# Final norm's factors and the last rows' residual sums in PSUM instead of SBUF

## The chip, the cores and the metric

The kernel runs on one core of one Trainium2 chip. The metric is the device time of one execution in microseconds. A core has TensorE (PE; its weight loads are listed as PEld), VectorE (DVE), ScalarE (ACT), GpSimd (POOL), SyncE (SP, here only an issuer of DMAs), an on-chip memory SBUF of 128 partitions, and PSUM, which holds the results of TensorE in 8 banks of 512 float32 numbers per partition.

## The reference, cut to what matters

The model is one step of a two-layer streaming encoder: a gated short convolution, then multi-head latent attention, each with a norm before it and a residual add behind it, and one norm at the end. There are 1024 prompt frames and 64 sample frames, which the kernel handles as 1088 columns of width 1024. What the change touches is the end of layer 2, the residual sum and the final norm:

```
def rms_norm(x, g):
    y = x * rsqrt(mean(x * x, axis=-1) + EPS)
    return y * g

yp = (silu(zp) * op) @ mla_w_out      # 1024 x 1024
xp = xp + yp                          # residual sum
y_prompt = rms_norm(xp, final_norm_g) # the same for the sample frames
```

## The kernel before

Nearly everything is a float32 product made of three matmuls on operands that are split into a high and a low part (`hi`, `lo`): hi·hi, hi·lo, lo·hi. A weight block arrives by DMA (`wraw`, or `xraw`), ACT writes its high part (`whi`), and POOL subtracts to get the low part (`wlo`, or `xlo`); blocks 0 and 1 below have their lower half split between POOL and DVE.

The stage that matters is the last one, the output projection. It has two parts.

- Columns 0 to 831 are kept transposed, with the 1024 features in 8 groups of 128 partitions (`dt`), and in two column groups, (448, 832) and (0, 448). For every `dt`, PE makes one sum per column group in one of the four PSUM banks 0 to 3 that `gps()` hands out in turn, DVE adds the residual into `X2` (L1841), ACT squares it (L1846), DVE adds up the squares in `acc1` (L1848), and ACT multiplies `X2` by the norm's weight (L1853). After the last `dt`, the generator `finish` turns the summed squares into factors: PE sums over partitions with a matrix of ones, `wide_rstd` forms the factors rf (ACT Ln and Exp at L363 and L364, one correction step at L365 to L367), and then DVE multiplies all 8 slices of `X2` by rf (L1737) and SP sends each slice out (L1738). There are 8 multiplies of 384 columns and 8 of 448.
- The last 256 columns are computed the other way round, as rows: two blocks `b` of 128 frames, each in two halves `h` of 512 features, in the four PSUM banks 4 to 7 (`acc[b][h]`). Their weights come in 8 blocks `e`, 0 to 3 for the first half and 4 to 7 for the second. `rows(e, w, b)` issues 6 matmuls. Blocks 0 to 5 are used for both `b` one after the other; then come blocks 6 and 7 for b=0, then 6 and 7 for b=1. `half_end(b, h)` ends a half: DVE adds the residual that was copied to `XG` (L1803; for b=1, h=1 PE has added it already), ACT squares and sums it (L1805), DVE multiplies by the norm's weight (L1806). At h=1 follow the factor of each row (L1810 to L1815), the scaling on three engines (L1816, L1817, L1819), and the output DMAs.

Both parts run interleaved: `advance()` moves the open `finish` generators one step per weight block. The order on each engine is the one in which the program was laid out by its scheduler; engines wait for each other through semaphores and never change that order. PE's order is pinned to the program's. The high parts `whi` have two buffers, so block 7's high part takes the buffer of block 4 and can be written only when PE has finished with block 4.

Of the kernel before, what the change touches and what calls it, by code (L numbers as in the profile page):

```python
# [14 lines left out]
AF = mybir.ActivationFunctionType  # L15
# [4 lines left out]
D = 1024  # L20
# [189 lines left out]
def kernel(ctx, tc, xT, small, w1, w2, w3, w3r, wpair, wqr, wv, wkT, w4,  # L210
# [3 lines left out]
    V, A, G, PE, SP = nc.vector, nc.scalar, nc.gpsimd, nc.tensor, nc.sync  # L214
# [9 lines left out]
    def nm(s):  # L224
        cnt[0] += 1
        return f"{s}_{cnt[0]}"
# [9 lines left out]
    def gps(tag="g", size=1):  # L236
        (b0, b1), k = turns[tag]
        turns[tag][1] = (k + size) % (b1 - b0)
        return PS[:, b0 + k:b0 + k + size, :].rearrange("p b n -> p (b n)")
# [27 lines left out]
    def ordered(ins):  # L267
        if keep_order[0]:
            tc.keep_in_program_order(ins)
# [29 lines left out]
    def mm(ps, lhsT, rhs, start, stop, more=False):  # L299

        ins = PE.matmul(ps, lhsT, rhs, start=start, stop=stop, skip_group_check=more)  # L301
        if pe_order[0]:
            tc.keep_in_program_order(ins)
# [45 lines left out]
    def wide_split(hi, lo, acc, eps):  # L349

        ordered(A.activation(out=hi, in_=acc, func=AF.Identity, bias=eps))
        ordered(V.scalar_tensor_tensor(lo, acc, eps, r32(hi), op0=ALU.add, op1=ALU.subtract))

    def wide_sum(hi, lo, n, tag="g"):

        ps = gps(tag)[:, :n]
        mm(ps, onesr, hi, True, False)
        mm(ps, onesr, lo, False, True)
        return ps

    def wide_rstd(out, ps, n, t):

        tc.keep_in_program_order(A.activation(out=t, in_=ps, func=AF.Ln, scale=1.0 / n))  # L363
        tc.keep_in_program_order(A.activation(out=out, in_=t, func=AF.Exp, scale=-0.5))  # L364
        ordered(A.activation(out=t, in_=out, func=AF.Square))  # L365
        ordered(V.scalar_tensor_tensor(t, t, -0.5 / n, ps, op0=ALU.mult, op1=ALU.mult))
        ordered(V.scalar_tensor_tensor(out, t, 1.5, out, op0=ALU.add, op1=ALU.mult))  # L367
# [98 lines left out]
    def conv_mm(c, W, lag=0, mid=None):  # L466

        cs = slice(c * NS, (c + 1) * NS)
        wh, wl = W
        ps = gps()[:, :NS]  # L470
        for k in range(KD + lag):
            if k == KD // 2 and mid:
                mid()
            if k < KD:
                mm(ps, wh[:, k * P:(k + 1) * P], HS[:, k, cs], k == 0, False)
                mm(ps, wh[:, k * P:(k + 1) * P], LS[:, k, cs], False, False)
            if k >= lag:
                mm(ps, wl[:, (k - lag) * P:(k - lag + 1) * P], HS[:, k - lag, cs], False, k == KD + lag - 1)
        return ps
# [318 lines left out]
    for ct in range(STD):  # L798
# [70 lines left out]
        else:  # L869
            for pi, part in enumerate(PARTS):  # L870
# [4 lines left out]
                for c in range(2):  # L875
                    ps = conv_mm(c, W, (KD, 0)[c])
# [59 lines left out]
    for dt in range(KD):  # L936
# [5 lines left out]
        for c, (c0, c1) in enumerate(CHK):  # L942
            n = c1 - c0
            x = xr[c]
            ps = gps()
# [103 lines left out]
    def latent_mm(f, c):  # L1049
        c0, c1 = CHK[c]  # L1050
        if c == 0:
            lat[f] = load_w(w3[f], 1024)
        ps = gps("z")[:, :c1 - c0]
        xg(ps, *lat[f], c0, c1)
        return ps
# [39 lines left out]
    ps = latent_mm(2, 0)  # L1095
    q_rstd(1, sq1)
    latent_evac(2, 0, ps)
    ps = latent_mm(2, 1)
# [48 lines left out]
    for c, (c0, c1) in enumerate(CHK):  # L1147
        n = c1 - c0
        ps = gps("z")
# [115 lines left out]
    for g in range(4):  # L1265
# [3 lines left out]
        if g == 2:  # L1269
            ps = gps()  # L1270
# [405 lines left out]
    OS, W4 = {}, {}  # L1676
# [39 lines left out]
    GB = po.tile([P, D], F32, name="GB")  # L1716
# [7 lines left out]
    def finish(c0, c1, sq):  # L1724

        n = c1 - c0
        rf = acc1[:, c0:c1]
        V.tensor_add(rf, rf, sq)
        wide_split(*OS[c0, 0], rf, eps_sum[D])
        yield  # L1730
        if c0 == 0:
            yield
        t = po.tile([P, 512], F32, tag="sq", name=nm("sq"), bufs=3)
        wide_rstd(rf, wide_sum(*OS[c0, 0], n), D, t[:, :n])
        yield
        for dt in range(KD):
            (G if dt in () else V).tensor_mul(X2[:, dt, c0:c1], X2[:, dt, c0:c1], rf)  # L1737
            SP.dma_start(out=o_y[dt][:, c0:c1], in_=X2[:, dt, c0:c1])  # L1738
            if dt in (1, 3, 5):
                yield  # L1740
# [28 lines left out]
    acc = [[PS[:, 4 + 2 * b + h, :] for h in range(2)] for b in range(2)]  # L1769
    Y = [XG.rearrange("p d n -> p (d n)")[:, b * D:(b + 1) * D] for b in range(2)]  # L1770
# [26 lines left out]
            mm(acc[b][h], ol[:, bs], wh[:, kk], False, q == 3 and kk == 1)  # L1797

    def half_end(b, h):
        yh = Y[b][:, 512 * h:512 * h + 512]  # L1800
        s0, s1, v0, v, t, y = [ss[:, 8 * b + i:8 * b + i + 1] for i in range(6)]
        if b * h == 0:
            V.tensor_add(yh, acc[b][h], yh)  # L1803
        junk = po.tile([P, 512], F32, tag="sq", name=nm("sq"), bufs=3)
        A.activation(out=junk, in_=acc[b][h] if b * h else yh, func=AF.Square, accum_out=s1 if h else s0)  # L1805
        V.tensor_mul(yh, acc[b][h] if b * h else yh, GB[:, 512 * h:512 * h + 512])  # L1806
        if h == 0:
            V.tensor_scalar(v0, s0, 1.0 / D, EPS, op0=ALU.mult, op1=ALU.add)
            return
        A.activation(out=t, in_=s1, func=AF.Ln, scale=1.0 / D, bias=v0)  # L1810
        A.activation(out=y, in_=t, func=AF.Exp, scale=-0.5)
        V.scalar_tensor_tensor(v, s1, 1.0 / D, v0, op0=ALU.mult, op1=ALU.add)
        V.tensor_mul(t, y, y)
        V.scalar_tensor_tensor(t, t, -0.5, v, op0=ALU.mult, op1=ALU.mult)
        V.scalar_tensor_tensor(y, t, 1.5, y, op0=ALU.add, op1=ALU.mult)  # L1815
        A.activation(out=Y[b][:, 0:256], in_=Y[b][:, 0:256], func=AF.Copy, scale=y)  # L1816
        G.tensor_scalar(Y[b][:, 256:512], Y[b][:, 256:512], y, 1.0, op0=ALU.mult, op1=ALU.mult)  # L1817
        (A if b else SP).dma_start(out=o_t[b][:, 0:512], in_=Y[b][:, 0:512])
        V.tensor_scalar(Y[b][:, 512:1024], Y[b][:, 512:1024], y, None, op0=ALU.mult)  # L1819
        SP.dma_start(out=o_t[b][:, 512:1024], in_=Y[b][:, 512:1024])  # L1820
# [3 lines left out]
    for dt in range(KD):  # L1824
        if dt == 7:
            raw_load(0)
        if dt == 4:
            residual()
        if dt > 1:
            W4[dt] = load_w(w4[dt], 1024)  # L1830
        wh, wl = W4[dt]
        x1 = po.tile([P, 832], F32, tag="x1", name=nm("x1"), bufs=2)
        SP.dma_start(out=x1, in_=x1_d[dt][:, :832])
        for c0, c1 in GRP[0]:
            n = c1 - c0
            ps = gps()
            gemm(ps[:, :n],
                 lambda k: wh[:, k * P:(k + 1) * P], lambda k: wl[:, k * P:(k + 1) * P],
                 lambda k: OS[c0, k][0], lambda k: OS[c0, k][1], KD)
            xs = X2[:, dt, c0:c1]  # L1840
            V.tensor_add(xs, ps[:, :n], x1[:, c0:c1])  # L1841
            if dt == 0:
                A.activation(out=acc1[:, c0:c1], in_=xs, func=AF.Square)
            else:
                q = po.tile([P, 512], F32, tag="sq", name=nm("sq"), bufs=3)
                A.activation(out=q[:, :n], in_=xs, func=AF.Square)  # L1846
                if dt < KD - 1:
                    V.tensor_add(acc1[:, c0:c1], acc1[:, c0:c1], q[:, :n])  # L1848
                else:
                    fins.append(finish(c0, c1, q[:, :n]))  # L1850
                    for x in fins[::-1]:
                        next(x)
            A.activation(out=xs, in_=xs, func=AF.Copy, scale=sm[:, C_FG + dt:C_FG + dt + 1])  # L1853
# [4 lines left out]
    for e in range(8):  # L1858
        if e + 2 + 1 < 8:
            raw_load(e + 2 + 1)  # L1860
            w.append(raw_split())
        for b in range(2) if e < 6 else ():
            rows(e, w[e], b)
            if e == 3:
                half_end(b, 0)
        advance()
    for b in range(2):
        for e in (6, 7):
            rows(e, w[e], b)
        half_end(b, 1)  # L1870
# [90 lines left out]
```

## Time and profile before

| | |
|---|---|
| time, median of 3 runs | 1099.64 us (1098.98 to 1100.81) |
| profiled execution's own time | 1099.2 us |
| span of its profile | 1097.4 us |
| busy: PE, DVE, ACT, POOL | 95%, 69%, 58%, 48% of the span |

PE is busy almost all the time and its granted clock is full in nearly all of the 40 slices of the page; only the last slice stands clearly apart (PE 4 tenths busy, clock 7 tenths). A busy share is an average over all stages, so it tells nothing of that last slice; for it one reads the waits and the timelines of 1060 to 1097 us, instruction by instruction.

### The profile page before, as it was taken

How to read it: one execution, taken by the hardware profiler on the slowest of the kernel's cores; microseconds unless marked ns; L12 is line 12 of the kernel's file. 1: busy time of each engine (PE TensorE's matmuls, PEld its weight loads, DVE VectorE, ACT ScalarE, POOL GpSimd, SP SyncE). 2: the span in 40 equal slices, each digit the busy share in tenths (PEclk: the TensorE clock that was granted, in tenths of full speed). 3: DMA queues.
4: the chain of work that ended last, by engine and by line, in shares of the span. 5: the costliest groups of instructions: out<-in, count | busy, mean ns of one | idle time of the engine just before them, and what ended most of it. 6: DMA issues, size and time to landing. Idle time of an engine off the chain costs nothing.

```text
span 1097.4 us, 19670 instructions
## 1 busy us (share of the span) xinstructions
PE 1048.0 (95%) x7123; PEld 1003.3 (91%) x7123; DVE 754.0 (69%) x1523; ACT 638.3 (58%) x1388; POOL 532.1 (48%) x446
## 2 busy tenths in 40 slices
PE   9989998989999999999899999999999999989994
PEld 8979998989999999999798999899999999879983
DVE  6888666756666445555996432788888888896456
ACT  5446676666666533345522334877787778785352
POOL 0475698886576622113452322445555545563243
PEclk9999999999999999999998999999999999999997
DMA  7244232442323244422142114433422331334224
GB/s 236 69 129 147 88 124 92 134 153 84 116 79 114 82 151 140 133 99 80 53 139 104 34 50 115 104 80 87 109 57 66 88 90 47 103 120 150 89 85 155
DMA packets 58145, 114.55 MB, mean 104 GB/s; under 512 B 8080, under 2 KB 32400, under 8 KB 58048
## 3 DMA queue, kind: packets, MB, share of 16 engines
q1 hardware_dynamic: 57840, 112.97, 33.7%
q8 instruction: 56, 0.92, 0.4%
q14 instruction: 41, 0.34, 0.1%
q10 hardware_dynamic: 144, 0.26, 0.1%
q0 software_dynamic: 64, 0.07, 0.0%
HBM read 79.27 MB, written 16.31 MB: 87 GB/s over the span
## 4 chain that ended last, share of the span: by engine, by line
PE 69%; DVE 10%; POOL 5%; issue 5%; DMA 4%; ACT 4%; SPq 1%; POOLq 0%; DVEq 0%; ACTq 0%
PE PS L301 48%; PE PS L1487 16%; PE PS L1526 5%; DMA QB<-stg 3%; POOL wlo L1765 1%; DMA wraw<-in_w 1%; POOL wlo L292 1%; DVE PS L488 1%; ACT PH L1539 1%; DVE OL L1011 1%; ACT stg L1603 1%; POOL R L565 1%; SPq L1613 1%; DVE PL L1543 0%; POOL R L513 0%
## 5 line engine op out<-in xcount | busy, mean ns | idle before, releaser
L301 PE MATMUL PS<-R,whi 128*128 128x272 f32 (+2 forms) x1662 | 370.4, 313 | 15.4 <-ACT whi L288 4.4
L301 PEld LDWEIGHTS PS<-R,whi 128*128 128x128 f32 x1662 | 276.6, 191 | 20.1 <-ACT whi L288 5.1
L301 PE MATMUL PS<-R,wlo 128*128 128x272 f32 (+2 forms) x888 | 265.9, 311 | 1.2 <-POOL wlo L292 1.2
L292 POOL TENSOR_TENSOR wlo<-wraw,whi 128x1024 fp32r<-128x1024 f32 x36 | 88.7, 2465 | 185.5 <-ACT whi L288 179.6
L301 PEld LDWEIGHTS PS<-R,wlo 128*128 128x128 f32 x888 | 164.1, 190 | 2.4 <-POOL wlo L292 1.9
L1487 PE MATMUL PS<-KB,QB 96*128 96x512 f32 (+11 forms) x576 | 125.2, 355 | 1.1 <-DVE SZ L1031 0.6
L1521 POOL TENSOR_SCALAR Pt<-Pt,st 128x640 f32<-128x640 f32 (+3 forms) x64 | 61.4, 961 | 86.4 <-DVE st L1517 85.9
L1487 PEld LDWEIGHTS PS<-KB,QB 96*128 96x128 f32 (+1 forms) x576 | 94.4, 190 | 9.4 <-DVE PL L1543 1.1
L1504 DVE TENSOR_REDUCE st<-PS 128x1 f32<-128x1024 f32 (+7 forms) x128 | 94.7, 748 | 10.9 <-PE PS L1487 10.2
L1543 DVE TENSOR_TENSOR PL<-PS,PH 128x512 fp32r<-128x512 f32 (+3 forms) x192 | 98.7, 547 | 3.1 <-ACT PH L1539 1.8
L1539 ACT CAST PH<-PS 128x512 fp32r<-128x512 f32 (+3 forms) x192 | 85.4, 497 | 14.7 <-PE PS L1526 13.5
L1487 PE MATMUL PS<-PH,VB 128*128 128x256 f32 x320 | 76.5, 279 | 0.0
L637 POOL TENSOR_TENSOR wlo<-wraw,whi 128x1024 fp32r<-128x1024 f32 x26 | 62.5, 2404 | 27.1 <-ACT whi L636 24.2
L1487 PE MATMUL PS<-PL,VB 128*128 128x256 f32 x320 | 75.3, 282 | 0.2 <-DVE PL L1543 0.2
L1513 ACT ACTIVATE Pt<-PS,st 128x640 f32<-128x640 f32 (+3 forms) x64 | 62.1, 970 | 5.7 <-DVE st L1517 2.6
L301 PE MATMUL PS<-R,bhi 128*128 128x272 f32 x320 | 61.1, 289 | 2.6 <-DVE z L763 1.0
L1487 PEld LDWEIGHTS PS<-PH,VB 128*128 128x128 f32 x320 | 60.8, 190 | 1.3 <-DVE PL L1543 0.8
L1487 PEld LDWEIGHTS PS<-PL,VB 128*128 128x128 f32 x320 | 61.1, 191 | 0.7 <-DVE PL L1543 0.4
L288 ACT CAST whi<-wraw 128x1024 fp32r<-128x1024 f32 (+1 forms) x37 | 38.2, 1033 | 38.3 <-PE PS L301 20.6
L1526 PE MATMUL PS<-ident,Pt 128*128 128x128 f32 x416 | 55.4, 274 | 0.2 <-ACT Pt L1513 0.2
L301 PEld LDWEIGHTS PS<-R,bhi 128*128 128x128 f32 x320 | 49.6, 188 | 3.7 <-DVE z L763 1.2
L1568 POOL TENSOR_TENSOR SZ<-SZ,ot 64x256 f32<-64x256 f32 x64 | 47.0, 746 | 11.7 <-DVE ot L1563 9.4
(438 smaller groups left out, 2623.0 us busy)
## 6 DMA issues: line engine op xcount, KB each, us to landing
wraw<-in_w SPq DMA_DIRECT2D x83, 512.0 KB, 3.6
KB<-stg SPq DMA_DIRECT2D x32, 256.0 KB, 3.8
QB<-stg SPq DMA_DIRECT2D x32, 256.0 KB, 4.7
braw<-in_w SPq DMA_DIRECT2D x13, 512.0 KB, 4.4
QB<-qr_scratch SPq DMA_DIRECT2D x32, 128.0 KB, 3.1
x<-x_scratch SPq DMA_DIRECT2D x8, 416.0 KB, 3.2
xr<-in_xT SPq DMA_DIRECT2D x16, 192.0 KB, 2.4
x_scratch<-xr SPq DMA_DIRECT2D x16, 192.0 KB, 1.9
```

Source lines behind the costliest of these rows:

```text
L288: ins = A.copy(out=hi[:, :n], in_=raw[:, :n])
L292: ins = (lo_engine or G).tensor_sub(lo[:, :m], raw[:, :m], r32(hi[:, :m]))
L301: ins = PE.matmul(ps, lhsT, rhs, start=start, stop=stop, skip_group_check=more)
L637: ins = eng.tensor_sub(lo, src, r32(hi))
L1487: pin(PE.matmul(ps, lhsT, rhs, start=start, stop=stop))
L1504: pin(V.tensor_reduce(out=st[:, 0:1], in_=TL["S", h, i], axis=AX.XY, op=ALU.max, negate=True))
L1513: pin(A.activation(out=Pt, in_=TL.pop(("S", h, i)), func=AF.Exp, bias=st[:, 0:1], accum_out=st[:, 1:2]))
L1521: pin(G.tensor_scalar(Pt, Pt, st[:, 2:3], 1.0, op0=ALU.mult, op1=ALU.mult))
L1526: pin(PE.transpose(out=tp[:, j * P:(j + 1) * P], in_=TL["P", h, i][:, (j0 + j) * P:(j0 + j + 1) * P], identity=ident))
L1539: pin(A.copy(out=hi, in_=src))
L1543: pin(V.tensor_sub(lo, src, r32(hi)))
L1568: pin(G.tensor_mul(sz, sz, TL.pop(("ot", h, pr))[rows]))
```

## The change

In `finish`, the factors rf are no longer written over `acc1` in SBUF but into a PSUM bank of their own, one more call of `gps()` per column group. The 16 multiplies of `X2` then read one operand from SBUF and one from PSUM. In `half_end`, the residual sum of the three halves that need it is written back into its PSUM bank instead of into `XG`; the square and the multiply by the norm's weight read it there. No instruction is added or removed.

```diff
--- before.py
+++ after.py
@@ -1731,7 +1731,9 @@
         if c0 == 0:
             yield
         t = po.tile([P, 512], F32, tag="sq", name=nm("sq"), bufs=3)
-        wide_rstd(rf, wide_sum(*OS[c0, 0], n), D, t[:, :n])
+        ps = wide_sum(*OS[c0, 0], n)
+        rf = gps()[:, :n]
+        wide_rstd(rf, ps, D, t[:, :n])
         yield
         for dt in range(KD):
             (G if dt in () else V).tensor_mul(X2[:, dt, c0:c1], X2[:, dt, c0:c1], rf)
@@ -1797,13 +1799,13 @@
             mm(acc[b][h], ol[:, bs], wh[:, kk], False, q == 3 and kk == 1)
 
     def half_end(b, h):
-        yh = Y[b][:, 512 * h:512 * h + 512]
+        yh, ps = Y[b][:, 512 * h:512 * h + 512], acc[b][h]
         s0, s1, v0, v, t, y = [ss[:, 8 * b + i:8 * b + i + 1] for i in range(6)]
         if b * h == 0:
-            V.tensor_add(yh, acc[b][h], yh)
+            V.tensor_add(ps, ps, yh)
         junk = po.tile([P, 512], F32, tag="sq", name=nm("sq"), bufs=3)
-        A.activation(out=junk, in_=acc[b][h] if b * h else yh, func=AF.Square, accum_out=s1 if h else s0)
-        V.tensor_mul(yh, acc[b][h] if b * h else yh, GB[:, 512 * h:512 * h + 512])
+        A.activation(out=junk, in_=ps, func=AF.Square, accum_out=s1 if h else s0)
+        V.tensor_mul(yh, ps, GB[:, 512 * h:512 * h + 512])
         if h == 0:
             V.tensor_scalar(v0, s0, 1.0 / D, EPS, op0=ALU.mult, op1=ALU.add)
             return
```

The scheduler lays the instructions out nearly as before. On DVE, from the correction of the first factors to the residual sums of the first halves, the kernel before has (`sq` is the scratch of the correction, `acc` the factors, `X` is `X2`):

```order
L366 SCALAR_TENSOR_TENSOR sq_12072<-sq_12072,PS 128x384
L367 SCALAR_TENSOR_TENSOR acc_100<-sq_12072,acc_100 128x384
L1737 TENSOR_TENSOR X_11529<-X_11529,acc_100 128x384 x5
L366 SCALAR_TENSOR_TENSOR sq_12139<-sq_12139,PS 128x448
L1737 TENSOR_TENSOR X_11529<-X_11529,acc_100 128x384
L367 SCALAR_TENSOR_TENSOR acc_100<-sq_12139,acc_100 128x448
L1737 TENSOR_TENSOR X_11529<-X_11529,acc_100 128x384
L1737 TENSOR_TENSOR X_11529<-X_11529,acc_100 128x448 x2
L1803 TENSOR_TENSOR XG<-PS,XG 128x512 x2
```

and the changed kernel, with two lines more in its numbering:

```order
L366 SCALAR_TENSOR_TENSOR sq_12072<-sq_12072,PS 128x384
L367 SCALAR_TENSOR_TENSOR PS<-sq_12072,PS 128x384
L1739 TENSOR_TENSOR X_11529<-X_11529,PS 128x384 x4
L366 SCALAR_TENSOR_TENSOR sq_12139<-sq_12139,PS 128x448
L1739 TENSOR_TENSOR X_11529<-X_11529,PS 128x384
L367 SCALAR_TENSOR_TENSOR PS<-sq_12139,PS 128x448
L1739 TENSOR_TENSOR X_11529<-X_11529,PS 128x384
L1739 TENSOR_TENSOR X_11529<-X_11529,PS 128x448 x2
L1805 TENSOR_TENSOR PS<-PS,XG 128x512 x2
```

The first run of multiplies is one shorter, the multiply that left it stands behind the first halves' end; what stands in front of the two residual sums is otherwise the same, and the operand `acc` has become `PS`.

On ACT, the stretch from the high part of block 5 (`xhi`) to the first square of the second half reads in the kernel before (`whi_12179` is block 6's high part, `whi_12215` block 7's):

```order
L1763 CAST xhi_12153<-xraw_12151 128x1024
L1763 CAST whi_12179<-wraw_12177 128x1024
L1805 ACTIVATE sq_12190,ss<-XG 128x512
L1805 ACTIVATE sq_12201,ss<-XG 128x512
L1763 CAST whi_12215<-wraw_12213 128x1024
L1805 ACTIVATE sq_12264,ss<-XG 128x512
```

and in the changed kernel:

```order
L1765 CAST xhi_12153<-xraw_12151 128x1024
L1765 CAST whi_12179<-wraw_12177 128x1024
L1807 ACTIVATE sq_12190,ss<-PS 128x512
L1807 ACTIVATE sq_12201,ss<-PS 128x512
L1765 CAST whi_12215<-wraw_12213 128x1024
L1807 ACTIVATE sq_12264,ss<-PS 128x512
```

Nothing moved: the two squares of the first halves stand in front of block 7's cast in both, and read PSUM now. The orders of PE and POOL are unchanged. On the SP queue the output of the last but one 384-column slice stands behind four outputs of 448 columns instead of in front of them.

## Rows read from the trace of the kernel before

**Rows 1.** Waits by engine and releaser, 1060 to 1098 us: total, times, longest

```profile
PE PS L301 <- POOL wlo L1765: 4.7, 1, 4.7
PE PS L301 <- ACT whi L1763: 4.4, 1, 4.4
```

**Rows 2.** Stretches: busy us of PE, PEld, DVE, ACT, POOL; granted clock; DMA

```profile
1072.60:1075.40 2.80, 2.80 (x13) 2.06 (x11) 2.80 (x7) 0.00 (x0) 0.00 (x0) 1.00 0.55 204
...
1085.40:1089.00 3.60, 3.57 (x8) 2.81 (x9) 0.69 (x1) 0.31 (x1) 0.00 (x0) 0.50 0.00 0
```

**Rows 3.** Timeline of PE: start, duration, instruction, idle before and releaser

```profile
1070.99 0.39 PE L301 MATMUL PS<-whi,OL 128*128 128x512 f32 x1
...
1075.12 0.40 PE L301 MATMUL PS<-whi,OL 128*128 128x512 f32 x1
1079.93 0.80 PE L301 MATMUL PS<-whi,OH 128*128 128x512 f32 x1 [4.42 <-ACT whi L1763]
1085.43 0.79 PE L301 MATMUL PS<-wlo,OH 128*128 128x512 f32 x1 [4.70 <-POOL wlo L1765]
...
1087.30 0.63 PE L301 MATMUL PS<-whi,OL 128*128 128x512 f32 x1
```

**Rows 4.** Timeline of POOL, 1039 to 1100 us

```profile
1039.48 2.40 POOL L292 TENSOR_TENSOR wlo<-wraw,whi 128x1024 fp32r<-128x1024 f32 x1 [6.70 <-ACT whi L288]
...
1062.10 5.09 POOL L1765 TENSOR_TENSOR wlo<-wraw,whi 128x1024 fp32r<-128x1024 f32 x2 [2.58 <-ACT whi L1763]
1067.16 2.72 POOL L1765 TENSOR_TENSOR xlo<-xraw,xhi 128x1024 fp32r<-128x1024 f32 x1
...
1079.96 5.42 POOL L1765 TENSOR_TENSOR wlo<-wraw,whi 128x1024 fp32r<-128x1024 f32 x1 [7.41 <-ACT whi L1763]
```

**Rows 5.** Timeline of ACT, 1040 to 1100 us

```profile
1077.61 0.63 ACT L1805 ACTIVATE sq<-XG 128x512 f32<-128x512 f32 x1 [7.89 <-DVE XG L1803]
...
1078.85 1.03 ACT L1763 CAST whi<-wraw 128x1024 fp32r<-128x1024 f32 x1
...
1090.70 0.51 ACT L1816 ACTIVATE XG<-XG,ss 128x256 f32<-128x256 f32 x1 [0.73 <-DVE ss L1815]
1091.32 0.60 ACT L1805 ACTIVATE sq<-PS 128x512 f32<-128x512 f32 x1
```

**Rows 6.** Timeline of DVE, 1040 to 1100 us

```profile
1063.03 0.56 DVE L366 SCALAR_TENSOR_TENSOR sq<-sq,PS 128x384 f32<-128x384 f32 x1 [1.61 <-ACT sq L365]
1063.62 1.30 DVE L367 SCALAR_TENSOR_TENSOR acc<-sq,acc 128x384 f32<-128x384 f32 x1
1064.96 8.94 DVE L1737 TENSOR_TENSOR X<-X,acc 128x384 f32<-128x384 f32 x5
...
1076.89 1.28 DVE L1803 TENSOR_TENSOR XG<-PS,XG 128x512 f32<-128x512 f32 x2
...
1079.95 3.22 DVE L1737 TENSOR_TENSOR X<-X,acc 128x448 f32<-128x448 f32 x6
1087.96 0.69 DVE L1803 TENSOR_TENSOR XG<-PS,XG 128x512 f32<-128x512 f32 x1 [4.79 <-PE PS L301]
...
1092.04 0.69 DVE L1806 TENSOR_TENSOR XG<-PS,GB 128x512 f32<-128x512 f32 x1 [0.85 <-ACT sq L1805]
```

**Rows 7.** DVE groups by shape, 940 to 1098 us: total busy, mean ns

```profile
L1841 DVE TENSOR_TENSOR X<-PS,x 128x384 f32<-128x384 f32 x8 | 4.5, 556 | 6.4 <-PE PS L301 6.4
...
L1806 DVE TENSOR_TENSOR XG<-XG,GB 128x512 f32<-128x512 f32 x3 | 2.0, 685 | 0.8 <-ACT sq L1805 0.8
...
L1806 DVE TENSOR_TENSOR XG<-PS,GB 128x512 f32<-128x512 f32 x1 | 0.7, 692 | 0.9 <-ACT sq L1805 0.9
```

**Rows 8.** One line, L1543, 900 to 960 us: ns min/median/max

```profile
L1543 DVE TENSOR_TENSOR PL<-PS,PH x40: 271/610/693, 901.6 to 959.6; 128x512 fp32r<-128x512 f32 x20, 128x256 fp32r<-128x256 f32 x7, 128x384 fp32r<-128x384 f32 x7, 128x128 fp32r<-128x128 f32 x6
```

**Rows 9.** Timeline of the SP queue, 1062 to 1086 us

```profile
1064.54 0.37 SPq L1751 DMA_DIRECT2D wraw<-in_w  x1
```

**Rows 10.** DMA issues, 1035 to 1098 us: count, KB, us to landing

```profile
wraw<-in_w SPq DMA_DIRECT2D x4, 512.0 KB, 3.5
```

## The prediction

> **What bounds the kernel now.** PE is busy 95% of the span, so the end can come earlier only if PE loses idle time or if the work behind its last matmul gets shorter. I read the waits of the last 40 us first. PE waits twice and long: 4.4 us for block 7's high part and 4.7 us for its low part [rows 1]. [...]
>
> The timelines then tell why block 7 is late; I follow it backwards.
>
> - Its low part is a POOL instruction that starts at 1079.96 and takes 5.42 us; a lone one of that size takes 2.40 [rows 4]. The difference is 3.0 us, and from 1079.95 on DVE runs six multiplies in 3.22 us [rows 6]: POOL got through only behind them.
> - Its high part is cast at 1078.85, behind the squares of the two first halves on ACT, the first of which waited 7.89 us for DVE's residual sum [rows 5].
> - That sum starts at 1076.89, because DVE had five multiplies of 384 columns in front that took 8.94 us, 1.79 each, while POOL made low parts without a break from 1062.10 on [rows 4, 6].
>
> What makes these multiplies slow is seen in three neighbouring rows. The correction at 1063.03 reads one operand from PSUM and takes 0.56 us with POOL at work. The next, of the same size but with both tensor operands in SBUF, takes 1.30; then come the multiplies, both operands in SBUF too [rows 4, 6]. The same pair of engines loses time both ways: DVE waits in 1063 to 1073, POOL waits at 1080. With one operand in PSUM nothing of it shows: the forty subtractions of the attention stage never exceed 0.693 us, the time of their largest shape [rows 8]. The change puts exactly the second operand of these multiplies into PSUM.
>
> **The change part by part.** Times are those of the profiled execution.
>
> 1. First factors. The 384-column correction starts as before at 1063.03. Its second instruction falls from 1.30 to about 0.56: the multiplies start at 1064.22 instead of 1064.96.
>
> 2. Multiplies in front of the residual sums: six of 384, two of 448, and the other correction's two instructions of 448. A multiply of an SBUF and a PSUM tensor is not in this trace; the nearest row is the add of PSUM and SBUF at 384 columns, 0.556 us [rows 7]. Back to back, instructions overlap by some 0.08: two residual sums take 1.28 us, one takes 0.69; six multiplies take 3.22, which is 0.54 each [rows 6]. I take 0.47 for 384 (0.556 less 0.08) and 0.54 for 448: 6 x 0.47 + 4 x 0.54 = 5.0 us. The residual sums can start at 1069.2; PE is ready for them (block 3's last matmul starts 12 x 0.23 before 1070.99, so it ends at 1068.6 [rows 3]). Bounds: no row of these shapes is closer than 0.47 and 0.54, so these are the floor too; without any overlap it is 0.56 and 0.62, some 5.8 us, and if POOL holds them up as before it is 11.9 (1064.96 to 1076.89).
>
> 3. Block 7's high part. Before, the cast came 1.96 us behind the first residual sum (1078.85 less 1076.89). That gives 1071.2. But it also needs the buffer of block 4, whose last matmul ends at 1070.99 + 0.39 = 1071.38. So PE, not DVE, releases it, at 1071.45. Its data are there: the load is issued at 1064.54 and lands some 3.5 us later [rows 9, 10].
>
> 4. Block 7's low part. Cast 1.05, hand-over 0.06, then 2.40 on POOL with no SBUF-only DVE instruction beside it: ready at 1075.0.
>
> 5. PE. Block 6's last matmul for b=0 starts at 1075.12, the first of block 7 follows at 1075.35 and the second, which needs the low part, at 1075.58. That is 0.6 us after it is ready, so both waits vanish, and with them the slow clock. Block 7's sixth matmul starts at 1076.52 instead of 1087.30 and ends 0.39 later; the residual sum of b=0, h=1 starts at 1076.94 instead of 1087.96. **That is 11.0 us.**
>
> 6. Is DVE free by then? Behind the first two sums it has two multiplies by the norm's weight and eight of `X2`: 1.28 + 1.3 + 6 x 0.54 + 2 x 0.47 + 0.2 for two tiny ones, from 1069.2 to about 1076.1. Yes, by 0.8 us. The output DMAs of the multiplies follow them and are out of the way some 4 us before the last rows' outputs.
>
> 7. The end. From that residual sum on, the chain is the old one: sum, square, Ln, Exp, three short DVE steps, scaling, square of b=1 at 1091.32, and 6.08 us from there to 1097.4. PE's last twelve matmuls end 2.74 us behind block 7's sixth, at 1079.7, before ACT is free for that square (1091.21 less 11.0 is 1080.2), so the chain on ACT and DVE sets the end, and up to 0.1 us is gained there. The sum and the square in PSUM instead of SBUF cost nothing that rows show: 685 and 692 ns for the multiply of either kind [rows 7].
>
> [...] The new operands would let the weight multiply of a half run beside its square, since neither writes what the other reads. The row at 1092.04 shows such a pair already: both read one PSUM bank, and the multiply waits 0.85 us for the square all the same [rows 6]. [...]
>
> The sum: 1097.4 - 11.0 - 0.05 = 1086.3 of span, 1088.1 for the profiled execution (1099.2 before). The median of the runs lay 0.44 above that execution, so I carry the 11.1 us over to it: 1099.64 - 11.1 = 1088.5; between the two I write 1088.4.
>
> **The rivals.**
>
> *DVE becomes the bound.* If multiplies with a PSUM operand do not overlap, or pay some 0.1 to 0.2 us each, DVE finishes the sixteen late. With 0.2 more each it reaches the first sums at 1070.8, past the 1070.1 up to which block 7's low part is still in time, and ends its queue at 1079.3 instead of 1076.1: the last sum comes 2.4 us late. The two delays overlap, so the time is about 1090.8. For it: the price of this form is not in the trace. Against: two sums with a PSUM operand do overlap [rows 6]. Chance 0.12.
>
> *POOL still holds them up.* If it is the multiply's own tile, read and written in SBUF, that collides with POOL, the change does not do what it says. Everything from 1064.96 on stays, less the 0.7 us of the corrected factors, which the chain may or may not hand on: 1098.9 to 1099.6. Against: L1543 and the correction at 1063.03 also read and write SBUF. Chance 0.05.
>
> *PSUM reads slow down.* The factors lie in banks beside the ones that PE writes. If DVE's reads there were slowed, all sixteen multiplies would stand in front of the last sum: with m us each it starts at 1064.2 + 16 m + 3.9 (corrections, two sums, weight multiplies). At m = 1.24 that is 1087.96, no change; from 1.38 on it is over 0.2% later than now, and at 1.5 it is 1092.1, so the time is 1103.8. For it: no row has this form. Against: 1.38 is two and a half times the 0.556 of rows 7, whose adds also read PSUM while PE writes the neighbour banks. Chance 0.03.
>
> **How the numbers follow.** The forecast has 0.80 and a range of its own of 1087.0 to 1089.6: down by the overlap in step 7 and half a microsecond of scatter, up by a block 7 that misses its 0.6 us of slack by a little. The range takes in the first rival: 1086.6 to 1091.5, which leaves out some 0.13. About 0.2% (2.2 us) is what a measurement can tell from no change. Faster: 0.80 + 0.12 = 0.92; same 0.05; slower 0.03.
>
> **What would show it.** In the new profile the 384-column multiplies between 1064 and 1069 take about 0.56 us each and the POOL low parts 2.4, not 2.7; the first residual sums start near 1069.2; block 7's cast follows block 4's last matmul at 1071.4 and its low part ends by 1075.0; PE has no gap of over 1 us after 1062, and its clock stays at 1.00 to its last matmul near 1079.5; the sum of b=0, h=1 starts near 1077. Multiplies of 1.8 us beside POOL would refute step 2 and with it the forecast; a sum of b=0, h=1 released by DVE's own queue and not by PE would be the first rival.

## The result and the profile after

The changed kernel takes 1087.35 us at the median (1086.35 to 1089.01, 4 runs) against 1099.8 us (1098.98 to 1100.81, 4 runs) for the kernel before. The ratio is 0.9888 with a 95% interval of 0.9871 to 0.9905. The profiled execution took 1086.63 us, its span is 1084.8. One of the six runs of the kernel with the factors only, in the table below, took 1303.64 us at a granted clock of 0.721, where the others had 0.98 or more; it is left out of that kernel's numbers.

Start with DVE. This is its timeline in the changed kernel: start, duration, instruction, and the idle time before it.

```profile
1061.70 0.56 DVE L366 SCALAR_TENSOR_TENSOR sq<-sq,PS 128x384 f32<-128x384 f32 x1 [1.54 <-ACT sq L365]
1062.29 0.56 DVE L367 SCALAR_TENSOR_TENSOR PS<-sq,PS 128x384 f32<-128x384 f32 x1
1062.88 1.95 DVE L1739 TENSOR_TENSOR X<-X,PS 128x384 f32<-128x384 f32 x4
...
1066.28 1.61 DVE L1739 TENSOR_TENSOR X<-X,PS 128x384 f32<-128x384 f32 x3
1067.80 1.29 DVE L1805 TENSOR_TENSOR PS<-PS,XG 128x512 f32<-128x512 f32 x2
...
1070.85 3.67 DVE L1739 TENSOR_TENSOR X<-X,PS 128x448 f32<-128x448 f32 x7
1075.67 0.70 DVE L1805 TENSOR_TENSOR PS<-PS,XG 128x512 f32<-128x512 f32 x1 [1.15 <-PE PS L301]
1077.12 0.69 DVE L1808 TENSOR_TENSOR XG<-PS,GB 128x512 f32<-128x512 f32 x1 [0.75 <-ACT sq L1807]
```

The second instruction of the 384-column correction takes 0.56 us where it took 1.30, and four multiplies take 1.95 us, 0.49 each, where five took 8.94, 1.79 each [rows 6]. From the first multiply to the first residual sum it is 4.92 us instead of 11.93, with one multiply fewer in between. The groups by shape show where the gain lies (total busy, mean ns), first the changed kernel, then the kernel before:

```profile
L1739 DVE TENSOR_TENSOR X<-X,PS 128x448 f32<-128x448 f32 x8 | 4.6, 613 | 0.0
L1739 DVE TENSOR_TENSOR X<-X,PS 128x384 f32<-128x384 f32 x8 | 4.1, 548 | 0.0
```

```profile
L1737 DVE TENSOR_TENSOR X<-X,acc 128x384 f32<-128x384 f32 x8 | 10.6, 1362 | 0.0
L1737 DVE TENSOR_TENSOR X<-X,acc 128x448 f32<-128x448 f32 x8 | 4.6, 615 | 0.0
```

Only the multiplies of 384 columns were slow on DVE. Those of 448 were not: three ran while POOL was idle, and beside the six of [rows 6], five of them of 448 columns, it was POOL that lost time.

POOL's timeline: two low parts take 4.79 where they took 5.09, and block 7's, the last, takes 2.41 where it took 5.42 [rows 4].

```profile
1060.82 4.79 POOL L1767 TENSOR_TENSOR wlo<-wraw,whi 128x1024 fp32r<-128x1024 f32 x2 [2.58 <-ACT whi L1765]
1065.68 2.42 POOL L1767 TENSOR_TENSOR xlo<-xraw,xhi 128x1024 fp32r<-128x1024 f32 x1
1068.52 2.41 POOL L1767 TENSOR_TENSOR wlo<-wraw,whi 128x1024 fp32r<-128x1024 f32 x1 [0.41 <-ACT whi L1765]
1071.32 2.41 POOL L1767 TENSOR_TENSOR wlo<-wraw,whi 128x1024 fp32r<-128x1024 f32 x1 [0.39 <-ACT whi L1765]
```

ACT's timeline: block 7's cast comes 1.65 us behind the start of the first square and ends five microseconds before the next square, which waits for DVE's sum [rows 5].

```profile
1068.53 0.60 ACT L1807 ACTIVATE sq<-PS 128x512 f32<-128x512 f32 x1
...
1070.18 1.05 ACT L1765 CAST whi<-wraw 128x1024 fp32r<-128x1024 f32 x1 [0.37 <-issue]
1076.40 0.60 ACT L1807 ACTIVATE sq<-PS 128x512 f32<-128x512 f32 x1 [5.16 <-DVE PS L1805]
...
1078.37 0.51 ACT L1818 ACTIVATE XG<-XG,ss 128x256 f32<-128x256 f32 x1 [0.72 <-DVE ss L1817]
1078.79 0.58 ACT L1807 ACTIVATE sq<-PS 128x512 f32<-128x512 f32 x1
```

And PE, from block 4's last matmul to its own last one:

```profile
1069.71 0.39 PE L301 MATMUL PS<-whi,OL 128*128 128x512 f32 x1
...
1074.07 0.40 PE L301 MATMUL PS<-whi,OH 128*128 128x512 f32 x1
1074.30 0.39 PE L301 MATMUL PS<-wlo,OH 128*128 128x512 f32 x1
...
1075.24 0.39 PE L301 MATMUL PS<-whi,OL 128*128 128x512 f32 x1
...
1078.04 0.40 PE L301 MATMUL PS<-whi,OL 128*128 128x512 f32 x1
```

Block 7's first two matmuls follow each other after 0.23 us; both waits of [rows 1] are gone, and no matmul of the stage is at the slow clock of [rows 2], 0.50: from 1062.0 to 1078.4 the granted clock is 1.00. In the chain that ended last, followed from 1040 us on, PE's matmuls now reach without a break up to the residual sum of b=0, h=1 (start, length, what):

```profile
1039.84 35.81 PE PS L301 x169
...
1075.67 0.71 DVE PS L1805
...
1076.40 0.70 ACT sq L1807 x2
```

**How much of the 12.45 us is the change's?** The two profiles already stand apart in code that is the same in both: the 384-column correction starts at 1063.03 in one and at 1061.70 in the other. From that instruction to the end it is 34.37 us before and 23.10 after. So in these two profiles the last part is 11.27 us shorter. The other 1.33 us of the two spans lie ahead of it, where PE, DVE, ACT and POOL run the same instructions in the same order in both. Only ACT's last steps there write and read the factors in PSUM already, and DVE waits 1.54 us for them instead of 1.61 [rows 6]. The next section asks whether the rest is a gain. I call the part from the correction's start to the end of the span the last stretch and use it beside the times.

### The profile page after: what moved, and what is told of

The parts are those of the page before. It is cut to its first block, busy times and chain, and to the rows that moved or that the text cites. A ratio compares the mean times of both kernels' runs of the same rounds, so it can differ in the third digit from the quotient of the medians.

```text
span 1084.8 us, 19669 instructions
## 1 busy us (share of the span) xinstructions
PE 1045.5 (96%) x7123; PEld 1002.3 (92%) x7123; DVE 746.9 (69%) x1523; ACT 638.2 (59%) x1388; POOL 528.4 (49%) x446
## 4 chain that ended last, share of the span: by engine, by line
PE 74%; DVE 11%; ACT 4%; POOL 3%; DMA 3%; issue 3%; SPq 1%; POOLq 0%; DVEq 0%; ACTq 0%
PE PS L301 52%; PE PS L1487 17%; PE PS L1526 5%; DMA QB<-stg 2%; DVE PS L488 1%; POOL wlo L292 1%; DVE OL L1011 1%; ACT PH L1539 1%; ACT stg L1603 1%; POOL R L565 1%; POOL R L513 0%; DMA wraw<-in_w 0%; DVE qt L1212 0%; DVE SZ L367 0%; SPq L1613 0%
## 5 line engine op out<-in xcount | busy, mean ns | idle before, releaser
L1543 DVE TENSOR_TENSOR PL<-PS,PH 128x512 fp32r<-128x512 f32 (+3 forms) x192 | 98.7, 547 | 3.1 <-ACT PH L1539 1.8
```

The source lines that it names most:

```text
L1543: pin(V.tensor_sub(lo, src, r32(hi)))
```

## The experiments

The theory: a DVE instruction with two tensor operands in SBUF and a low part on POOL exclude each other; the multiplies lost their time so, and with the factors in PSUM they no longer do. The rivals: the factors' own place (they no longer overwrite `acc1`), the order on DVE, the residual sums, or a tile in SBUF that is slow in itself. Each kernel was timed against the kernel before on its own chip; the last stretch is from its profile.

| kernel | us, median | kernel before | ratio, 95% interval | last stretch, us |
|---|---|---|---|---|
| before | | | | 34.37 |
| changed | 1087.35 | 1099.8 | 0.9888 (0.9871 to 0.9905) | 23.10 |
| changed, again | 1086.1 | 1099.23 | 0.9875 (0.9853 to 0.9897) | 23.12 |
| factors only | 1088.72 | 1099.23 | 0.9899 (0.9874 to 0.9925) | 25.36 |
| sums only | 1099.34 | 1099.23 | 0.9997 (0.9982 to 1.0013) | 34.75 |
| factors in an SBUF tile of their own | 1099.56 | 1099.23 | 0.9996 (0.9981 to 1.0010) | 34.68 |
| order alone | 1095.53 | 1100.11 | 0.9961 (0.9947 to 0.9975) | 29.53 |
| PSUM for 384 columns only | 1094.39 | 1100.11 | 0.9946 (0.9933 to 0.9959) | 27.63 |
| POOL idle | 1093.1 | 1100.11 | 0.9937 (0.9919 to 0.9954) | 27.75 |
| changed, other ending | 1087.57 | 1100.11 | 0.9884 (0.9870 to 0.9898) | 22.85 |

**The changed kernel again**, without an edit.

> The changed kernel once more, for the distance to the kernel before on one chip and for the scatter of its unchanged part. Theory (the gain is the collision of VectorE and GpSimd on two SBUF operands, gone): about 11.3 us faster (10.96 us up to the residual sum of b=0, h=1 and 0.3 us behind it), so near 1088; the 384-column multiplies take 0.55 us each. The start of the 384-column correction (1063.03 in the profile before, 1061.70 in the first profile after) lies in unchanged code and is expected to differ by about 1 us from execution to execution. Rival (the other 1.3 us of the first result is a gain too): the correction starts at 1061.7 again and the gain is 12.4.

The last stretch is 23.12 us, the same to 0.02. But the correction started at 1065.28 this time, 3.6 us later than in the first profile. In the unchanged code such shifts come and go (1060.42 to 1065.28 over the ten profiles of this study), so one pair of profiles tells nothing of 1.3 us. On the mean the correction starts at 1062.9 in the five profiles with the 384-column factors in PSUM and at 1062.8 in the other five: no gain ahead of it shows. The times do not exclude one. This kernel is 13.13 us faster than the kernel before, where some 11.3 were expected, and the three timings with the whole change give 12.45, 13.13 and 12.54 us, all above 11.27, with intervals that begin at 10.4, 11.3 and 11.2. So 11.27 us are traced to the change; whether up to 2 us more are its work or scatter stays open.

**Factors only.** `half_end` is as before.

```diff
     def half_end(b, h):
-        yh, ps = Y[b][:, 512 * h:512 * h + 512], acc[b][h]
+        yh = Y[b][:, 512 * h:512 * h + 512]
...
-            V.tensor_add(ps, ps, yh)
+            V.tensor_add(yh, acc[b][h], yh)
...
```

> Only the final norm's factors go to PSUM; the last rows' sums stay in SBUF. Theory: the multiplies of X2 are as fast as in the changed kernel (0.55 us), so most of the gain is here. But the two weight multiplies of the first halves read XG and GB in SBUF, and now fall beside POOL's low part of block 6: DVE waits up to 1.4 us for it, then block 7's low part or the second weight multiply waits as well. So 0.2 to 2.3 us more than the changed kernel: 1088 to 1090. Rival (the two parts of the change are independent and the second is worth nothing): the same time as the changed kernel within 0.2 us and weight multiplies of 0.69 us.

The multiplies of 384 columns are as fast as in the changed kernel (0.546 us), but the last stretch is 2.26 us longer. DVE's and POOL's timelines show where:

```profile
1069.37 1.99 DVE L1808 TENSOR_TENSOR XG<-XG,GB 128x512 f32<-128x512 f32 x1
...
1071.34 2.83 DVE L1808 TENSOR_TENSOR XG<-XG,GB 128x512 f32<-128x512 f32 x1
...
1077.73 0.68 DVE L1805 TENSOR_TENSOR XG<-PS,XG 128x512 f32<-128x512 f32 x1
```

```profile
1068.40 2.41 POOL L1767 TENSOR_TENSOR wlo<-wraw,whi 128x1024 fp32r<-128x1024 f32 x1 [0.42 <-ACT whi L1765]
1071.20 2.42 POOL L1767 TENSOR_TENSOR wlo<-wraw,whi 128x1024 fp32r<-128x1024 f32 x1 [0.39 <-ACT whi L1765]
```

The weight multiplies of the first halves, both operands in SBUF again, take 1.99 and 2.83 us instead of 0.68. POOL's two low parts end at 1070.81 and 1073.62, and each multiply ends 0.55 us behind one of them, as if it had waited for POOL. Behind them DVE ends late, and the sum of b=0, h=1 starts at 1077.73, right behind DVE's own queue. So the second half of the change is worth 2.3 us, but only together with the first: it keeps a collision away that the earlier start of these multiplies would bring. The difference of the times, 2.6 us, goes the same way but lies within their intervals.

**Sums only.** The factors stay in `acc1`.

```diff
-        ps = wide_sum(*OS[c0, 0], n)
-        rf = gps()[:, :n]
-        wide_rstd(rf, ps, D, t[:, :n])
+        wide_rstd(rf, wide_sum(*OS[c0, 0], n), D, t[:, :n])
```

> Only the last rows' sums go to PSUM; the factors stay in acc1 in SBUF. Theory: the multiplies in front of the first residual sums still collide with POOL, 1.8 us each on the mean, and the first sums start some 13.8 us behind the correction as before: no change, 1099 to 1100. Rival (the sums carry part of the gain): 1 us or more faster.

No change, as the theory expected; here, as in the kernel before, the weight multiplies of the first halves meet an idle POOL and take 0.68 us each.

**Factors in an SBUF tile of their own.**

```diff
-        rf = gps()[:, :n]
+        rf = po.tile([P, 832], F32, tag="x1", name=nm("rf"), bufs=2)[:, :n]
```

> As the changed kernel, but the factors go into an SBUF tile of their own instead of a PSUM bank. Theory (PSUM matters): the multiplies take 1.8 us each beside POOL, the time is that of the kernel before, 1099 to 1100. Rival (what matters is that the factors no longer overwrite acc1, which other instructions use): the multiplies take 0.55 us and the time is 1087 to 1088.

The whole gain is gone, and the timeline of DVE is that of the kernel before:

```profile
1061.02 1.30 DVE L367 SCALAR_TENSOR_TENSOR rf<-sq,rf 128x384 f32<-128x384 f32 x1
1062.35 8.94 DVE L1739 TENSOR_TENSOR X<-X,rf 128x384 f32<-128x384 f32 x5
```

Five multiplies take 8.94 us once more. What counts is the memory, not that `acc1` is left alone.

**Order alone.** Everything in SBUF as before, but the multiplies wait for the residual sums of the first halves.

```diff
         wide_rstd(rf, wide_sum(*OS[c0, 0], n), D, t[:, :n])
         yield
+        for _ in range(3 if c0 else 1):
+            yield
         for dt in range(KD):
-            (G if dt in () else V).tensor_mul(X2[:, dt, c0:c1], X2[:, dt, c0:c1], rf)
+            with tc.issue_after(last_on["sum"]):
+                V.tensor_mul(X2[:, dt, c0:c1], X2[:, dt, c0:c1], rf)
...
-            V.tensor_add(yh, acc[b][h], yh)
+            last_on["sum"] = V.tensor_add(yh, acc[b][h], yh).ins
```

> Factors and sums stay in SBUF as before, but the sixteen multiplies are laid out behind the two residual sums of the first halves (they wait for the second of these), so that the squares and block 7's cast no longer queue behind them. Theory (two SBUF operands on VectorE and POOL's low parts exclude each other): block 7's cast comes as early as PE allows, but the multiplies then meet POOL's low parts of blocks 6 and 7 and one side waits for the other: either POOL for up to 8 us or DVE for 2.7 us per multiply. The end comes 3 to 9 us later than in the changed kernel: 1090 to 1096. Rival (only the order on DVE mattered, the squares behind the multiplies): as fast as the changed kernel, 1086 to 1088.

It gains 0.39%, about a third of what the changed kernel gains, and lies in the range of the theory. PE no longer waits for block 7 at all, but the collision has moved with the multiplies:

```profile
1071.22 2.77 DVE L1740 TENSOR_TENSOR X<-X,acc 128x448 f32<-128x448 f32 x1
1073.91 2.89 DVE L1809 TENSOR_TENSOR XG<-XG,GB 128x512 f32<-128x512 f32 x1
...
1076.79 7.57 DVE L1740 TENSOR_TENSOR X<-X,acc 128x448 f32<-128x448 f32 x15
1084.28 0.68 DVE L1806 TENSOR_TENSOR XG<-PS,XG 128x512 f32<-128x512 f32 x1
```

```profile
1070.79 5.45 POOL L1768 TENSOR_TENSOR wlo<-wraw,whi 128x1024 fp32r<-128x1024 f32 x2
```

One multiply takes 2.77 us and one weight multiply 2.89 beside POOL's last two low parts; the other fifteen run at 0.50 each as soon as POOL is through, but too late: the last sum waits for them until 1084.28. The order explains how the lost time reached PE, not why it was lost.

**PSUM for the 384-column factors only.**

```diff
-        rf = gps()[:, :n]
+        rf = gps()[:, :n] if c0 else rf
```

> As the changed kernel, but only the 384-column factors are in PSUM; the 448-column ones stay in acc1. Theory: the six 384-column multiplies in front take 0.55 us, so the first sum starts about 5 us behind the correction; the 448-column multiplies meet POOL's blocks 5 to 7 with both operands in SBUF and cost DVE or POOL 2 us apiece where they meet: 1.5 to 5 us later than the changed kernel, 1088 to 1092. Rival (the collision is met only by the multiplies in front of the first sums): the time of the changed kernel within 0.5 us.

The last stretch is 4.53 us longer than the changed kernel's, inside the 1.5 to 5 that were expected. The median of the times, 1094.39, lies 2.4 above the upper end that I gave. The profiled execution, 1091.86, does not, but it is the shortest of the five. I put the difference down to the scatter of the code ahead, without a profile that shows it. On DVE each kind shows its own price; POOL's lines stand below:

```profile
1063.65 2.41 DVE L1739 TENSOR_TENSOR X<-X,PS 128x384 f32<-128x384 f32 x5
...
1066.98 2.35 DVE L367 SCALAR_TENSOR_TENSOR acc<-sq,acc 128x448 f32<-128x448 f32 x1
...
1069.85 1.14 DVE L1739 TENSOR_TENSOR X<-X,acc 128x448 f32<-128x448 f32 x2
...
1072.18 5.08 DVE L1739 TENSOR_TENSOR X<-X,acc 128x448 f32<-128x448 f32 x2
```

```profile
1061.59 4.79 POOL L1767 TENSOR_TENSOR wlo<-wraw,whi 128x1024 fp32r<-128x1024 f32 x2 [2.58 <-ACT whi L1765]
1066.44 2.41 POOL L1767 TENSOR_TENSOR xlo<-xraw,xhi 128x1024 fp32r<-128x1024 f32 x1
1071.68 5.11 POOL L1767 TENSOR_TENSOR wlo<-wraw,whi 128x1024 fp32r<-128x1024 f32 x2 [2.83 <-ACT whi L1765]
```

Five multiplies with a PSUM operand take 2.41 us beside POOL. The one 448-column correction with both operands in SBUF takes 2.35 beside POOL, and two multiplies of that kind 5.08. Two more of the same kind, from 1069.85 on, fall into the gap in which POOL is idle and take 1.14 together.

**POOL idle.** Everything in SBUF as before, but DVE makes the low parts of blocks 3 to 7.

```diff
-        for eng, a, b in ((G, 0, 512), (V, 512, 1024)) if e < 2 else ((G, 0, 1024),):
+        for eng, a, b in ((G, 0, 512), (V, 512, 1024)) if e < 2 else ((V if e >= 3 else G, 0, 1024),):
```

> Factors and sums in SBUF as before, but the low parts of blocks 3 to 7 are made by DVE instead of POOL, so POOL is idle while DVE multiplies. Theory: the multiplies with both operands in SBUF take 0.55 us (384) and 0.61 us (448), none over 0.7, as there is nothing to collide with. DVE pays five low parts of 1.1 to 1.2 us for it, block 7's comes about 3 us too late for PE, and the time is 1089 to 1094. Rival (an SBUF factor tile is slow in itself in this stage, by its address or by PE's and DMA's traffic): the multiplies in front of the first sums still take 1.8 us on the mean.

This is the cleanest test, since the multiplies are the very same instructions as before (total busy, mean ns):

```profile
L1737 DVE TENSOR_TENSOR X<-X,acc 128x448 f32<-128x448 f32 x8 | 4.6, 618 | 0.0
L1737 DVE TENSOR_TENSOR X<-X,acc 128x384 f32<-128x384 f32 x8 | 4.2, 551 | 0.0
```

At 384 columns it is 551 ns with both operands in SBUF and POOL idle, 1362 ns in the kernel before with POOL at work, and 548 in the changed kernel with a PSUM operand and POOL at work. The SBUF factors are not slow in themselves. POOL's low parts both read and write SBUF, and no run has a POOL instruction there that does only one of the two, so which of them collides is not shown. The kernel pays for its low parts on DVE, as expected: PE waits 2.8 us for block 7's.

```profile
PE PS L301 <- DVE wlo L1765: 2.8, 1, 2.8
```

**Another ending.** In the changed kernel, DVE takes over ACT's and POOL's shares of the last scaling for b=0, and ACT takes over POOL's for b=1.

```diff
-        A.activation(out=Y[b][:, 0:256], in_=Y[b][:, 0:256], func=AF.Copy, scale=y)
-        G.tensor_scalar(Y[b][:, 256:512], Y[b][:, 256:512], y, 1.0, op0=ALU.mult, op1=ALU.mult)
+        if b:
+            A.activation(out=Y[b][:, 0:512], in_=Y[b][:, 0:512], func=AF.Copy, scale=y)
+        else:
+            V.tensor_scalar(Y[b][:, 0:512], Y[b][:, 0:512], y, None, op0=ALU.mult)
```

> The changed kernel with another sharing of the last scaling: for b=0 DVE scales all 1024 columns and ACT none, so that ACT is free for b=1's square when PE ends; for b=1 ACT scales 512 columns, DVE 512 and POOL none. Expected from the profile of the changed kernel: the square of b=1 starts at PE's end, 0.3 us earlier, and the last scaling ends 0.2 us earlier (0.61 us on ACT for 0.77 on POOL): 23.1 us from the correction to the end become 22.6, which the times cannot tell from no change. Rival: DVE's two scalings for b=0 stand in front of b=1's weight multiply and take the gain back: 23.0 to 23.2.

The last stretch is 0.25 us shorter, half of the 0.5 expected: the square of b=1 is released by PE now, but ACT's 512 columns take 0.72 us, not 0.61. The times cannot tell it from the changed kernel.

```profile
1080.32 0.60 ACT L1807 ACTIVATE sq<-PS 128x512 f32<-128x512 f32 x1 [0.82 <-PE PS L301]
...
1082.30 0.72 ACT L1819 ACTIVATE XG<-XG,ss 128x512 f32<-128x512 f32 x1 [0.72 <-DVE ss L1817]
```

## Why the prediction was right

The forecast was 1088.4 us, the median is 1087.35, inside the range and inside the forecast's own range of 1087.0 to 1089.6. The steps below explain 0.17 of the 1.05 us between the two; the rest is not in the sum. The second timing of the changed kernel, 1086.1, lies even under the range's lower end of 1086.6. So the mechanism was right, but how well the number fits is in part luck: runs of one kernel scatter by some microseconds. By its steps:

1. First factors: 0.56 us for the second instruction of the correction, as said.
2. Multiplies: 4.92 us up to the first sum for the 5.0 of the sum, 548 ns each for the 556 that I took from the nearest row. Here a PSUM operand cost nothing more: with one it is 548 ns, with two SBUF operands and POOL idle 551. They also overlap alike: in a row, each further one adds 0.47 us with a PSUM operand (four take 1.95) and 0.48 with two SBUF operands and POOL idle (two take 1.03). Why the multiplies were slow at all is told by DVE's rows beside POOL: 2.66 to 2.76 us with two SBUF operands, 0.55 with one. The multiplies, corrections and weight multiplies of all ten profiles divide in the same way: with one operand in PSUM none takes more than 0.69 us, beside POOL's low parts or not; with both in SBUF they take at most 0.69 us while POOL is idle and 1.28 to 2.89 beside a low part, or the low part loses the time, as beside the six of [rows 6].
3. Block 7's cast starts 0.08 us behind the end of block 4's last matmul, which is at 1070.10. The trace names no releaser for it ("issue"), so that this matmul releases it is read from the times; in the second profile of the changed kernel the distance is 0.08 us too.
4. Its low part: 2.41 us, ready at 1073.73.
5. PE reaches the matmul that needs it at 1074.30: 0.57 us of slack for the 0.6 forecast, no wait. From the correction to the sum of b=0, h=1 it is 13.97 us instead of 24.93: 10.96 for the 11.0 of the sum.
6. DVE is free 1.15 us before that sum, for the 0.8 that I worked out; the sum is released by PE, and the multiplies overlap, which excludes the first rival.
7. The end: mis-sized, if only a little. I gave up to 0.1 us; it was 0.31 (9.44 before and 9.13 after from the sum's start). Before, the square of b=1 still waited for PE, whose matmuls had been slow up to 1089 (granted clock 0.50 [rows 2]), and started 0.62 us behind the start of ACT's scaling [rows 5]. Now PE is done at 1078.44 and the square starts 0.42 us behind that scaling, at 1078.79, as soon as ACT lets it. That is 0.20 of the 0.31 us, where the working had counted 0.11; the other 0.11 are spread over the steps before and behind it. The weight multiply at 1077.12 waits 0.75 us for the square that reads the same bank, though neither writes it, and nothing was gained there; before it was 0.85 us [rows 6].

The sum is thus 11.27 us where I had 11.1. One thing the working did not see, though its number came out right: it priced the weight multiplies at 0.65 us each and said that sums in PSUM instead of SBUF cost nothing. Moved forward beside POOL's low parts they would have cost 2.3 us with the sums in SBUF, as the kernel with the factors only shows. The edit that I valued at nothing protects the gain of the other.

The two rivals on the far side are excluded by the multiplies' 548 ns. That POOL still holds them up would have shown as in the kernel with the factors in an SBUF tile of their own, and slow reads of PSUM beside PE's writes show nowhere.

## What to carry to other kernels

Where VectorE and GpSimd work at the same time, look at the operands of VectorE's long two-tensor instructions. Here, with both in SBUF, they and GpSimd's took turns; with one in a free PSUM bank they ran side by side, each as fast as alone (548 ns a multiply of 384 columns for 551 with POOL idle, 2.41 us a low part for 2.40). Follow the price through the queues before you judge it. An engine that is 69% busy lost some 7.2 us (three multiplies of 2.66, 2.76 and 2.74 us for 0.55 each, and a correction of 1.30 for 0.56), and POOL lost 3.0 behind six multiplies. That became 9 us of idle time and a slow clock (0.50) on the engine that sets the end, because a cast stood behind a square that stood behind a sum that stood behind the multiplies. And when work moves forward, check what it runs beside in its new place. The same collision still stands elsewhere in the changed kernel: the sum of squares of 448 columns at 1038.63 (L1850, both operands in SBUF) takes 2.45 us beside a POOL low part.

## What the runs showed of the hardware that was not expected

- The two engines did not yield alike. This is the line of the `X2` multiplies in the kernel before, while POOL has four low parts to make (ns min/median/max):

```profile
L1737 DVE TENSOR_TENSOR X<-X,acc x9: 546/615/2762, 1065.0 to 1076.4; 128x384 f32<-128x384 f32 x7, 128x448 f32<-128x448 f32 x2
```

  Most take 0.6 us, but three of the first five take 2.66 to 2.76, about the length of one POOL low part each, and three of POOL's four parts take 2.70 to 2.73 instead of 2.40: a waiting DVE instruction got in behind every POOL instruction and ended 0.4 us behind it. A waiting POOL instruction did not get in between six DVE multiplies that followed each other without a gap: block 7's low part took 3.0 us more than alone, about the length of the stream [rows 4, 6]. The two other kernels with this order on DVE show the same (5.45 us). This is read from the traces, not tried by itself.
- Two SBUF operands are not the only case. The last scalings on DVE (L1821 in the changed kernel, `TENSOR_SCALAR`) read one tensor in SBUF, and POOL scales its share beside them. From the kernel with POOL idle, whose last scalings POOL still shares:

```profile
1083.99 0.48 POOL L1817 TENSOR_SCALAR XG<-XG,ss 128x256 f32<-128x256 f32 x1 [23.82 <-DVE ss L1815]
1087.43 0.77 POOL L1817 TENSOR_SCALAR XG<-XG,ss 128x256 f32<-128x256 f32 x1 [2.96 <-DVE ss L1815]
```

  The first meets no scaling on DVE and takes 0.48 us. The second starts 0.06 us behind one on DVE and takes 0.77, as do all that start so in the other profiles but the one with the order alone, where POOL's two take 1.38 together. In the kernel with the order alone DVE loses time too: two scalings in a row take 1.10 us beside POOL's two, where two in a row take 0.89 in the kernel with the other ending, in which POOL scales nothing.

```profile
1087.62 1.10 DVE L1822 TENSOR_SCALAR XG<-XG,ss 128x512 f32<-128x512 f32 x2
1087.68 1.38 POOL L1820 TENSOR_SCALAR XG<-XG,ss 128x256 f32<-128x256 f32 x2 [11.43 <-DVE ss L1818]
```

  This too is read from the traces; no kernel of this study changes it alone.
- After the two waits the slow clock lasted differently long in executions with the same waits (4.4 and 4.7 us in both): the matmuls, 0.43 us apart behind the waits, were back at 0.23 us apart from 1089.3 on in the kernel before and from 1089.8 on with the sums alone in PSUM, where the correction starts at 1063.05 for 1063.03. That is most of the 0.38 us between their last stretches.
- ACT's scaling of 512 columns took 0.72 us, where its squares of 512 take 0.58 to 0.63.
